# Part of a SwiGLU in-projection computed by seven block products over both token blocks, with weight loads of single pieces

## The chip, the core and the metric

The kernel runs on one core of a Trainium2 chip. The metric is the device time of one execution in microseconds. Time before: median 969.24 us of three runs (968.96 to 971.36).

## What is computed

A trunk of two layers on 256 tokens of width 1024, all in float32. Each layer is an FFN, a token mixer and a second FFN, each between two RMSNorms; layer 0 mixes by stick-breaking attention, layer 1 by latent attention with a rotary part. The FFN is what the change touches:

```python
def rms_norm(x, g):
    y = xf * lax.rsqrt(jnp.mean(xf * xf, axis=-1, keepdims=True) + EPS)
    return y * g

def swiglu(x, w_in, w_out):                       # w_in (1024, 2*2816), w_out (2816, 1024)
    gate, up = jnp.split(x @ w_in, 2, axis=-1)
    return (jax.nn.silu(gate) * up) @ w_out

f = swiglu(rms_norm(x, g[0]), ffn_w_in[i, 0], ffn_w_out[i, 0])
x = x + FFN_RESIDUAL_WEIGHT * rms_norm(f, g[1])   # then the mixer, then the second FFN
```

## The kernel before, in words

The 256 tokens are two blocks of 128. Every weight is streamed once from HBM in pieces of 128 rows by up to 512 columns. Precision is kept by taking each operand apart: ACT copies a piece, rounded, to a high part (L345, `split`), DVE subtracts that from the piece to get the low part (L351), and PE makes three products of a piece, high by high, low weight by high token and high weight by low token (`mm3`, recorded at L474). `use` (L585) is these three matmuls for one block; a piece is used by block 0 and later by block 1, then its two `r` slots come free.

An FFN (`ffn`, L617) goes over 11 tiles of 256 columns of gate beside the same 256 of up. For a tile, `project` (L595) sums eight pieces in a PSUM bank; ACT takes SiLU of the gate half, scaled by the norm's factor `rpre` (L634), DVE multiplies it with the scaled up half (L636), PE transposes the product (L482), ACT and DVE take it apart (L492, L512), and `out_rows` multiplies it with four pieces of the second weight into two banks that stay for the whole FFN. `pre_norm` (L547) transposes x, multiplies by the gain (L559) and takes the result apart; the norm's factor per token, from two squares on ACT (L540), a sum on DVE (L542) and a power on POOL (L544), is worked out beside it, since only L634 and L636 need it. `post_norm` (L569) scales the output and adds it to x (L578, L581).

The order of all instructions comes from a list scheduler (`Plan.run`, L167): every operation is recorded with an engine, a planned duration and what it reads and writes, and the scheduler places them with finite pools of slots: 76 `r` slots for operand parts, 9 `w` slots for intermediate tiles, 4 `raw` buffers of two pieces each for loads, 8 PSUM banks. Small operations (class 0) go ahead of the stream of pieces (class 1). On PE, block 0 may lead block 1 by a number of pieces that `LEADS` gives for each sub-layer; `CAPS` says how many pieces may be held ready. The loads go through SP's queue in the order of the pieces, each when its raw buffer is free.

## Time and profile before

| | |
|---|---|
| three runs | 969.24 us median (968.96 to 971.36) |
| profiled execution | span 968.2 us; the page gives no other time for it |
| PE, DVE, ACT busy | 956.9, 643.3, 562.7 us |
| granted TensorE clock | 1.00 in every slice, 0.999 in the mean |
| HBM read | 168.15 MB, 175 GB/s over the span, 276 to 280 in the first twentieth |

The span is cut off at the first and the last instruction of the core. Busy shares are averages over stages; the chain of waits tells what the end of the run hung on, and the groups by line tell what the pieces of it cost.

### The profile page before, as it was taken

What the parts mean: (1) busy time and instruction counts of PE and PEld (TensorE: products, weight loads), DVE (VectorE), ACT (ScalarE), POOL (GpSimd) and SP (SyncE); (2) the same over time, 40 slices, a digit from 0 to 9 for tenths busy, and PEclk for the clock granted to TensorE, in tenths of its full rate; (3) what the DMA queues carried; (4) which work ended last, traced back from release to release, by engine and by line L of the source; (5) the groups of instructions that cost most, each with busy time, mean ns of one, the idle gap of its engine ahead of it and who ended that gap; (6) DMA issues with size and microseconds to landing.
All of it is one profiled execution on the core that took longest, in us unless ns stands there. A gap on an engine that the chain in (4) does not pass through costs nothing.

```text
span 968.2 us, 13457 instructions
## 1 busy us (share of the span) xinstructions
PE 956.9 (99%) x4575; PEld 797.1 (82%) x4575; DVE 643.3 (66%) x1214; ACT 562.7 (58%) x1202; POOL 26.2 (3%) x75
## 2 busy tenths in 40 slices
PE   8999999999999999999999999999999999999997
PEld 6778888888888888888888888888899988888885
DVE  7884646678777875645477564556899997555533
ACT  7754535568878764545364453545798776444421
POOL 2000000000000000000000000000200000000000
PEclk9999999999999999999999999999999999999999
DMA  8885665634434385656745656575614178666511
GB/s 276 280 249 184 193 199 184 207 131 153 131 109 153 112 276 176 193 180 188 225 131 174 190 184 192 179 232 168 192 41 131 32 236 278 196 194 188 186 62 44
DMA packets 127974, 170.10 MB, mean 176 GB/s; under 512 B 8768, under 2 KB 109472, under 8 KB 127904
## 3 DMA queue, kind: packets, MB, share of 16 engines
q1 hardware_dynamic: 127792, 169.18, 55.2%
q8 instruction: 36, 0.59, 0.3%
q14 instruction: 34, 0.28, 0.1%
q10 hardware_dynamic: 112, 0.05, 0.0%
HBM read 168.15 MB, written 1.05 MB: 175 GB/s over the span
## 4 chain that ended last, share of the span: by engine, by line
PE 92%; DMA 3%; DVE 2%; ACT 1%; issue 1%; POOL 0%; SPq 0%; DVEq 0%; POOLq 0%; ACTq 0%
PE bank L474 88%; PE bank L482 5%; DMA raw<-in_ffn_w_in_dram 3%; DVE r L351 2%; ACT r L345 1%; SPq L334 0%; DVE w L636 0%; DVE w L559 0%; ACT r L492 0%; DVE x L581 0%; DVEq L1133 0%; ACT junk L540 0%; POOLq L1133 0%; POOL cbuild L299 0%; POOL invf L818 0%
## 5 line engine op out<-in xcount | busy, mean ns | idle before, releaser
L474 PE MATMUL bank<-r,r 128*128 128x512 f32 (+3 forms) x4080 | 926.2, 384 | 0.3 <-ACT r L345 0.2
L474 PEld LDWEIGHTS bank<-r,r 128*128 128x128 f32 (+1 forms) x4080 | 736.7, 188 | 139.5 <-ACT r L345 1.2
L351 DVE TENSOR_TENSOR r<-raw,r 128x512 fp32r<-128x512 f32 (+1 forms) x628 | 400.1, 683 | 42.4 <-ACT r L345 33.1
L345 ACT CAST r<-raw 128x512 fp32r<-128x512 f32 (+1 forms) x628 | 353.9, 616 | 56.8 <-DMA raw<-in_ffn_w_in_dram 26.7
L634 ACT ACTIVATE w<-bank,rpre 128x256 f32<-128x256 f32 x88 | 41.7, 474 | 215.5 <-PE bank L474 215.4
L636 DVE SCALAR_TENSOR_TENSOR w<-bank,rpre,w 128x256 f32<-128x256 f32 x88 | 42.5, 483 | 185.9 <-ACT w L634 185.9
L492 ACT CAST r<-bank 128x256 fp32r<-128x256 f32 (+5 forms) x166 | 64.2, 399 | 75.6 <-PE bank L482 65.7
L512 DVE TENSOR_TENSOR r<-bank,r 128x256 fp32r<-128x256 f32 (+5 forms) x166 | 74.3, 454 | 45.8 <-ACT r L492 44.7
L482 PE MATMUL bank<-ident,w 128*128 128x128 f32 (+1 forms) x326 | 55.0, 272 | 2.1 <-DVE w L636 2.0
L482 PEld LDWEIGHTS bank<-ident,w 128*128 128x128 f32 (+1 forms) x326 | 41.3, 137 | 16.6 <-DVE w L636 4.0
L512 DVE TENSOR_TENSOR r<-w,r 128x512 fp32r<-128x512 f32 x48 | 32.5, 687 | 4.9 <-ACT r L507 2.0
L540 ACT ACTIVATE junk<-bank 128x512 bf16<-128x512 f32 x24 | 14.3, 597 | 22.6 <-PE bank L474 22.5
L578 DVE TENSOR_TENSOR w<-bank,w 128x512 f32<-128x512 f32 x24 | 16.4, 684 | 15.9 <-ACT junk L540 15.7
L544 POOL TENSOR_TENSOR rpost<-ms,half_neg 128x1 f32<-128x1 f32 x12 | 6.6, 548 | 700.0 <-DVE ms L542 700.0
L559 DVE TENSOR_TENSOR w<-bank,gT 128x512 f32<-128x512 f32 x24 | 16.3, 686 | 2.2 <-PE bank L482 2.0
L540 ACT ACTIVATE junk<-x 128x512 bf16<-128x512 f32 x24 | 15.1, 631 | 4.3 <-DVE x L581 2.3
L581 DVE SCALAR_TENSOR_TENSOR x<-w,rpost,x 128x512 f32<-128x512 f32 x24 | 17.1, 745 | 0.4
L482 PE MATMUL bank<-ident,x 128*128 128x128 f32 x96 | 15.0, 297 | 0.0
L482 PEld LDWEIGHTS bank<-ident,x 128*128 128x128 f32 x96 | 12.9, 155 | 1.9 <-issue 0.2
L492 ACT CAST r<-w 128x512 fp32r<-128x512 f32 x20 | 12.2, 619 | 3.6 <-DVE w L559 3.5
L1035 ACT ACTIVATE w<-bank,mx 128x128 f32<-128x128 f32 (+1 forms) x32 | 13.1, 425 | 0.4 <-DVE mx L1031 0.3
L736 DVE SCALAR_TENSOR_TENSOR w<-bank,w 128x512 f32<-128x512 f32 x12 | 8.2, 689 | 4.3 <-ACT w L734 4.1
(85 smaller groups left out, 211.5 us busy)
## 6 DMA issues: line engine op xcount, KB each, us to landing
raw<-in_ffn_w_in_dram SPq DMA_DIRECT2D x352, 256.0 KB, 3.9
...
```

The lines of the kernel that those rows point to most:

```text
L345: h = op("act", act_us(n), lambda: nc.scalar.copy(pc.hi[:, :n], raw[:, off:off + n]), r=rr, w=[(pc.hi, 0)], cls=1, after=splits[-1:], piece=i)
L351: nc.vector.tensor_tensor(out=pc.lo[:, :n], in0=raw[:, off:off + n], in1=pc.hi[:, :n].bitcast(F32), op=ALU.subtract)
L474: nc.tensor.matmul(o, a, b, start=start, stop=stop, skip_group_check=True)
L482: nc.tensor.transpose(o, i, ident[:])
L492: nc.scalar.copy(dst(), src())
L512: nc.vector.tensor_tensor(out=dst(), in0=src(), in1=hi().bitcast(F32), op=ALU.subtract)
L540: op("act", act_us(512, 1), lambda src=src, h=h: nc.scalar.activation(junk[:], src(), AF.Square, scale=scale, accum_out=ss[:, h:h + 1]), r ...
L559: op("dve", dve_us(512), lambda h=h, y=y, tr=tr: nc.vector.tensor_tensor(out=y[:].rearrange("p (k t) -> p k t", t=P), in0=tr[:].rearrange( ...
L578: op("dve", dve_us(512), lambda h=h, t=t: nc.vector.tensor_mul(out=t[:], in0=acc[h][:], in1=g[h][:]), r=[(acc[h], 0), (g[h], 0)], w=[(t, 0 ...
L581: op("dve", dve_us(512) + 0.06, lambda h=h, t=t: nc.vector.scalar_tensor_tensor(xt[b][h][:], t[:], k.rpost[:], xt[b][h][:], op0=ALU.mult, ...
L634: op("act", act_us(FT, 1), lambda o=o, hid=hid: nc.scalar.activation(hid[:, 0:FT], o[:, 0:FT], AF.Silu, scale=k.rpre[:]), r=[(o, 0), (k.rp ...
L636: op("dve", dve_us(FT) + 0.06, lambda o=o, hid=hid: nc.vector.scalar_tensor_tensor(hid[:, FT:], o[:, FT:], k.rpre[:], hid[:, 0:FT], op0=AL ...
```

## The change

Two groups of 512 columns of gate and the same 512 of up, 1024 of the 2816, are computed together for both blocks of tokens as a two-by-two block product: tokens by halves of the 1024 inputs, inputs by gate and up. In Strassen's form (the variant with 15 sums) this takes seven block products instead of eight. Each product (`pair_product`) has four pieces, each used once, for both blocks at the same time. For them

- four sums of token operands are made for each FFN (`combos`, DVE), and taken apart by ACT and DVE;
- for each group 16 weight pieces are loaded, DVE makes 16 sums of pieces in place (`total`), and 28 pieces are taken apart instead of 16;
- two PSUM banks gather several products one after another, and ACT copies or DVE sums take the states in between out (`copy_act`, `vec512`).

Since tokens of both blocks are added to each other, the norm's factor must be in them before: `pre_norm` with `scaled=True` works out the factor first, ACT scales x by it (L627 of the changed kernel), and only then come the transposes; SiLU and product lose the factor. The remaining seven tiles, the seven products and the second weight are put in an order by `FFN_ORDER`. Loads take one piece each, into slots of the `w` pool, which grows from 9 to 25 (the four raw buffers go); `r` shrinks from 76 to 68 slots. The stream holds 628 loads where it held 508, of the same bytes. `LEADS`, `CAPS` and other tables have new values, and `AHEAD`, `KEEP` and `RESERVE` limit loads and splits in the scheduler.

```diff
-LEADS = [14, 12, 9, 16, 17, 7]
-CAPS = [28, 29, 23, 22, 32, 23]
-RSLOTS = 76
-WSLOTS = 9
-RAWS = 4
-HOLD = 0.25
-STOCK = 5
+LEADS = [14, 10, 13, 17, 15, 8]
+CAPS = [28, 27, 23, 22, 23, 24]
+RESERVE = [4, 6, 4, 4, 2, 6]
+AHEAD = 9
+KEEP = 12
+RSLOTS = 68
+WSLOTS = 25
+HOLD = 0.26
+STOCK = 7
 X1_AT = 1
 WARM_A = 4
 WARM_B = 4
+PAIR = 512
+FFN_ORDER = ("i0 i1 o0 s0.0 s0.1 s0.2 s0.3 o1 s0.4 s0.5 s0.6 i2 i3 s1.0 t0.0 s1.1 t0.1 s1.2 t0.2 s1.3 t0.3 s1.4 o2 "
+             "s1.5 o3 s1.6 i4 t1.0 t1.1 i5 t1.2 t1.3 i6 o4 o5 o6")
...
+                    if o.first is not None and (
+                            o.first - self.split_pos >= AHEAD or
+                            len(self.free["w"]) < KEEP):
+                        continue
+                    if o.debt > 0 and (self.held >= CAPS[o.phase] or
+                                       len(self.free["r"]) - self.debt < 2 + RESERVE[o.phase]):
                         continue
                     cand.append((max(o.ready, self.slots_ready(o), self.bank_ready(o, e), at[e]), o))
...
-        raw = Buf("raw")
...
+    def load(view, src, size):
+        raw = Buf("w")
+        o = op("dma", size / 360e3, lambda: nc.sync.dma_start(view(raw), src), w=[(raw, 0)], cls=1, after=stream[-1:])
+        o.first, o.phase = len(pieces), phase[0]
+        stream.append(o)
         return raw
...
+    def add_pair(kind, w, q, c0, raws):
+        def fetch(nm):
+            c = c0 + (FF if nm[1] == "2" else 0)
+            raws[nm] = [add_rows(kind, w, (int(nm[0]) - 1) * 512, k, c, PAIR) for k in range(4)]
+        def total(dst, src, neg=False):
+            for d, t in zip(raws[dst], raws[src]):
+                def fn(d=d, t=t):
+                    if neg:
+                        nc.vector.scalar_tensor_tensor(d[:], d[:], -1.0, t[:], op0=ALU.mult, op1=ALU.subtract)
+                    else:
+                        nc.vector.tensor_add(out=d[:], in0=d[:], in1=t[:])
+                op("dve", dve_us(PAIR), fn, r=[(d, 0), (t, 0)], w=[(d, 0)], cls=1)
+        def parts(nm):
+            for k in range(4):
+                split(raws[nm][k], kind + (q, k), PAIR)
+        if q == 0:
+            fetch("11")
+            parts("11")
+        elif q == 1:
+            fetch("12")
+            total("11", "12")
+            parts("11")
+        elif q == 2:
+            fetch("22")
+            total("11", "22")
+            total("12", "22")
+            parts("11")
+        elif q == 3:
+            parts("22")
+        elif q == 4:
+            parts("12")
+        elif q == 5:
+            fetch("21")
+            total("11", "21", True)
+            parts("21")
+        else:
+            parts("11")
...
-        for j in range(NJ + 1):
-            if j < NJ:
-                add_in2(("in", l, f, j), ffn_w_in[l, f], j * FT, FF + j * FT, FT)
-            if j >= 1:
-                add_rows(("out", l, f, j - 1), ffn_w_out[l, f], (j - 1) * FT, (l, f, j) == (1, 1, NJ))
+        w, w2 = ffn_w_in[l, f], ffn_w_out[l, f]
+        raws = {}
+        last = [i for i in FFN_ORDER.split() if i[0] in "ot"][-1]
+        for item in FFN_ORDER.split():
+            kind, n = item[0], item[1:]
+            if kind == "i":
+                add_in2(("in", l, f, int(n)), w, FF, AT[item], FT)
+            elif kind == "o":
+                add_out(("out", l, f, int(n)), w2, AT["i" + n], item == last and (l, f) == (1, 1))
+            elif kind == "s":
+                p, q = n.split(".")
+                add_pair(("pair", l, f, int(p)), w, int(q), AT["s" + p], raws.setdefault(p, {}))
...
+    def pre_norm(b, l, i, scaled=False):
         k = blocks[b]
         gi = (l * 6 + i) * KC
-        k.xh, k.xl = [Buf("r"), Buf("r")], [Buf("r"), Buf("r")]
+        k.xh, k.xl, k.y = [Buf("r"), Buf("r")], [Buf("r"), Buf("r")], [Buf("w"), Buf("w")]
+        if scaled:
+            stats(b, 0)
         for h in range(2):
-            y, tr = Buf("w"), Buf("bank")
-            def turn(h=h, tr=tr):
+            y, tr = k.y[h], Buf("bank")
+            xs = xt[b][h]
+            if scaled:
+                xs = Buf("w")
+                op("act", act_us(512, 1), lambda h=h, xs=xs: nc.scalar.activation(
+                    xs[:], xt[b][h][:], AF.Copy, scale=k.rpre[:]), r=[(xt[b][h], 0), (k.rpre, 0)], w=[(xs, 0)])
+            def turn(xs=xs, tr=tr):
                 for c in range(4):
-                    transpose(tr[:, c * P:(c + 1) * P], xt[b][h][:, c * P:(c + 1) * P])
-            k.turned = op("pe", 4 * pe_us(P), turn, r=[(xt[b][h], 0)], w=[(tr, 0)])
+                    transpose(tr[:, c * P:(c + 1) * P], xs[:, c * P:(c + 1) * P])
+            k.turned = op("pe", 4 * pe_us(P), turn, r=[(xs, 0)], w=[(tr, 0)])
...
     def use(b, key, fn, o, r, n):
-        """The products of one piece of a weight."""
-        k = blocks[b]
+        k = blocks[b or 0]
         i = piece_at[key]
         pc = pieces[i]
         k.last = op("pe", 3 * pe_us(n), lambda: fn(pc.hi[:, :n], pc.lo[:, :n]),
-                    r=r + [(pc.hi, 0), (pc.lo, 0)], w=[(o, 0)], cls=1, after=[k.last] if k.last else [], blk=b, piece=i)
+                    r=r + [(pc.hi, 0), (pc.lo, 0)], w=[(o, 0)], cls=1,
+                    after=[q.last for q in ([k] if b is not None else blocks) if q.last],
+                    blk=(b,) if b is not None else (0, 1), piece=i)
         k.last.phase = phase_of[i]
+        if b is None:
+            blocks[1].last = k.last
...
+    def combos():
+        (a11, a12), (a21, a22) = blocks[0].y, blocks[1].y
+        (h11, h12), (h21, h22) = blocks[0].xh, blocks[1].xh
+        (l11, l12), (l21, l22) = blocks[0].xl, blocks[1].xl
+        a5, a6, a3, a7 = (Buf("w") for _ in range(4))
+        par = {}
+        for nm, d, x, y, o in (("a5", a5, a22, a21, ALU.subtract), ("a7", a7, a11, a21, ALU.add),
+                               ("a6", a6, a5, a11, ALU.subtract), ("a3", a3, a12, a6, ALU.add)):
+            op("dve", dve_us(512), lambda d=d, x=x, y=y, o=o: nc.vector.tensor_tensor(
+                out=d[:], in0=x[:], in1=y[:], op=o), r=[(x, 0), (y, 0)], w=[(d, 0)], cls=0.6)
+            h, lo = Buf("r"), Buf("r")
+            op("act", act_us(512), lambda d=d, h=h: nc.scalar.copy(h[:], d[:]), r=[(d, 0)], w=[(h, 0)], cls=0.6)
+            op("dve", dve_us(512), lambda d=d, h=h, lo=lo: nc.vector.tensor_tensor(
+                out=lo[:], in0=d[:], in1=h[:].bitcast(F32), op=ALU.subtract), r=[(d, 0), (h, 0)], w=[(lo, 0)], cls=0.6)
+            par[nm] = (h, lo)
+        return [(h11, l11), par["a5"], par["a6"], par["a3"], par["a7"], (h12, l12), (h22, l22)]
...
+    def pair_product(l, f, p, q, st):
+        if not st:
+            st.update(Z=Buf("bank"), W=Buf("bank"), Y=Buf("bank"), s1=Buf("w"), s2=Buf("w"), m5=Buf("w"))
+        o = {0: "Z", 1: "W", 2: "Z", 3: "W", 4: "Z", 5: "Y", 6: "Z"}[q]
+        first, last = q in (0, 1, 5), q in (6, 3, 5)
+        xh, xl = par_now[0][q]
+        o = st[o]
+        for kc in range(4):
+            c = slice(kc * P, (kc + 1) * P)
+            use(None, ("pair", l, f, p, q, kc), lambda wh, wl, c=c, kc=kc: mm3(
+                o[:], xh[:, c], xl[:, c], wh, wl, first and kc == 0, last and kc == 3), o, [(xh, 0), (xl, 0)], 512)
+        if q == 0:
+            copy_act(st["s1"], o, [(o, 0)], [(st["s1"], 0)])
+        elif q == 1:
+            copy_act(st["m5"], o, [(o, 0)], [(st["m5"], 0)])
+        elif q == 2:
+            copy_act(st["s2"], o, [(o, 0)], [(st["s2"], 0)])
+        elif q == 3:
+            st["up0"] = Buf("w")
+            vec512(st["up0"], o, st["s2"], ALU.subtract)
+        elif q == 4:
+            st["up1"] = Buf("w")
+            vec512(st["up1"], o, st["m5"], ALU.subtract)
+        elif q == 5:
+            g = Buf("w")
+            vec512(g, o, st["s1"], ALU.add)
+            pair_hidden(0, p, g, 1.0, st["up0"])
+        else:
+            pair_hidden(1, p, o, -1.0, st["up1"])
...
-    for b in range(NB):
-        for l in range(2):
-            ffn(b, l, 0)
+    for l in range(2):
+        ffn(l, 0)
+        for b in range(NB):
             if l == 0:
                 sb_mixer(b)
             else:
                 mla_mixer(b)
-            ffn(b, l, 1)
+        ffn(l, 1)
```

The rows of a listing below stand in the order in which an engine takes its instructions.

On DVE at the start of the program, from the low parts of block 0's tokens to the third low part of a weight (L351 before, L366 in the changed kernel; L559 and L634 are gain multiplications, L512 and L574 low parts of tokens, L738 sums of tokens and L742 their low parts). Before:

```order
L512 TENSOR_TENSOR r_62<-w_139,r_61 128x512
L512 TENSOR_TENSOR r_65<-w_140,r_63 128x512
L351 TENSOR_TENSOR r_67<-raw_146,r_64 128x512
L351 TENSOR_TENSOR r_69<-raw_146,r_66 128x512
L351 TENSOR_TENSOR r_71<-raw_147,r_68 128x512
L351 TENSOR_TENSOR r_72<-raw_147,r_70 128x512
L559 TENSOR_TENSOR w_141<-bank_155,gT 128x512
L542 TENSOR_SCALAR msx_203<-ssx_202 128x1
L559 TENSOR_TENSOR w_142<-bank_156,gT 128x512
L512 TENSOR_TENSOR r_75<-w_141,r_73 128x512
L351 TENSOR_TENSOR r_77<-raw_148,r_74 128x512
```

Now, from the low part of block 1's tokens on:

```order
L574 TENSOR_TENSOR r_77<-w_148,r_74 128x512
L738 TENSOR_TENSOR w_151<-w_138,w_148 128x512
L574 TENSOR_TENSOR r_80<-w_150,r_78 128x512
L738 TENSOR_TENSOR w_152<-w_150,w_148 128x512
L742 TENSOR_TENSOR r_83<-w_151,r_81 128x512
L738 TENSOR_TENSOR w_130<-w_152,w_138 128x512
L738 TENSOR_TENSOR w_131<-w_142,w_130 128x512
L742 TENSOR_TENSOR r_87<-w_152,r_85 128x512
L742 TENSOR_TENSOR r_89<-w_130,r_86 128x512
L366 TENSOR_TENSOR r_92<-w_133,r_66 128x512
L742 TENSOR_TENSOR r_94<-w_131,r_90 128x512
L366 TENSOR_TENSOR r_96<-w_134,r_68 128x512
```

Before, four low parts of weights stood between block 0's tokens and block 1's gain; now the first two stand ahead of all of this, and the third comes behind both blocks' tokens and seven of the eight operations for the sums.

On DVE where block 1 goes from the first mixer into the second FFN (L578 and L653 are the products of the post-norm, L581 and L656 the additions to x, L351 and L366 low parts of weights). Before:

```order
L351 TENSOR_TENSOR r_80<-raw_146,r_117 128x512
L351 TENSOR_TENSOR r_118<-raw_146,r_107 128x512
L351 TENSOR_TENSOR r_97<-raw_147,r_135 128x512
L578 TENSOR_TENSOR w_143<-bank_156,w_140 128x512
L542 TENSOR_SCALAR ms_200<-ss_199 128x1
L578 TENSOR_TENSOR w_139<-bank_157,w_141 128x512
L581 SCALAR_TENSOR_TENSOR x_189<-w_143,rpost_201,x_189 128x512
L581 SCALAR_TENSOR_TENSOR x_189<-w_139,rpost_201,x_189 128x512
L636 SCALAR_TENSOR_TENSOR w_137<-bank_152,rpre_198,w_137 128x256
L559 TENSOR_TENSOR w_144<-bank_151,gT 128x512
L542 TENSOR_SCALAR msx_203<-ssx_202 128x1
```

Now:

```order
L420 TENSOR_TENSOR w_146<-w_146,w_151 128x512
L366 TENSOR_TENSOR r_126<-w_142,r_82 128x512
L420 TENSOR_TENSOR w_151<-w_151,w_138 128x512
L653 TENSOR_TENSOR w_145<-bank_156,w_144 128x512
L604 TENSOR_SCALAR ms_204<-ss_203 128x1
L653 TENSOR_TENSOR w_140<-bank_158,w_148 128x512
L656 SCALAR_TENSOR_TENSOR x_193<-w_145,rpost_205,x_193 128x512
L656 SCALAR_TENSOR_TENSOR x_193<-w_140,rpost_205,x_193 128x512
L420 TENSOR_TENSOR w_142<-w_142,w_131 128x512
L710 TENSOR_TENSOR w_150<-bank_160,w_150 128x256
L366 TENSOR_TENSOR r_108<-w_149,r_89 128x512
L604 TENSOR_SCALAR msx_207<-ssx_206 128x1
```

Here the sums of weight pieces for the first group of products (L420) have come in among block 1's norms; in DVE's order some of them stand behind a row that waits for block 1.

On ACT at the same place (L540 and L602 squares, L345 and L359 high parts of weights, L492 and L554 high parts of others). Before:

```order
L540 ACTIVATE junk,ss_199<-bank_156 128x512
L540 ACTIVATE junk,ss_199<-bank_157 128x512
L634 ACTIVATE w_137<-bank_152,rpre_198 128x256
L540 ACTIVATE junk,ssx_202<-x_189 128x512 x2
L492 CAST r_129<-bank_155 128x256
L492 CAST r_82<-w_144 128x512
L492 CAST r_102<-w_145 128x512
L345 CAST r_123<-raw_147 128x512
L345 CAST r_136<-raw_148 128x512
L345 CAST r_65<-raw_148 128x512
L345 CAST r_78<-raw_149 128x512
```

Now:

```order
L602 ACTIVATE junk,ss_203<-bank_156 128x512
L359 CAST r_89<-w_149 128x512
L602 ACTIVATE junk,ss_203<-bank_158 128x512
L602 ACTIVATE junk,ssx_206<-x_193 128x512
L708 ACTIVATE w_150<-bank_160 128x256
L602 ACTIVATE junk,ssx_206<-x_193 128x512
L554 CAST r_71<-bank_155 128x256
L627 ACTIVATE w_153<-x_193,rpre_208 128x512
L627 ACTIVATE w_152<-x_193,rpre_208 128x512
L554 CAST r_76<-w_139 128x512
L554 CAST r_84<-w_134 128x512
```

Between the squares of x (`ssx`) and the rounding of the normed tokens there are now two scalings (L627) that read the factor.

## Rows read from the trace of the kernel before

**Rows 1.** Part 1 of the page: busy us (share of the span) and instructions of each engine.

```profile
PE 956.9 (99%) x4575; PEld 797.1 (82%) x4575; DVE 643.3 (66%) x1214; ACT 562.7 (58%) x1202; POOL 26.2 (3%) x75
```

**Rows 2.** Chain that ended last, in order of time: start us, us, what.

```profile
81.54 14.99 PE bank L474 x66
98.36 14.99 PE bank L474 x66
```

**Rows 3.** Groups by line, PE: form, count | busy us, mean ns | idle before.

```profile
L474 PE MATMUL bank<-r,r 128*128 128x512 f32 x3672 | 870.8, 393 | 0.3 <-ACT r L345 0.2
```

**Rows 4.** Timeline, DVE, start of the run: start us, us, what.

```profile
15.84 3.09 DVE L351 TENSOR_TENSOR r<-raw,r 128x512 fp32r<-128x512 f32 x5
23.55 3.69 DVE L351 TENSOR_TENSOR r<-raw,r 128x512 fp32r<-128x512 f32 x6
```

**Rows 5.** Groups by line, DVE and ACT, columns as in rows 3.

```profile
L351 DVE TENSOR_TENSOR r<-raw,r 128x512 fp32r<-128x512 f32 x612 | 391.9, 686 | 41.8 <-ACT r L345 32.4 <-ACT w L731 0.6 <-PE bank L474 0.6
L636 DVE SCALAR_TENSOR_TENSOR w<-bank,rpre,w 128x256 f32<-128x256 f32 x88 | 42.5, 483 | 185.9 <-ACT w L634 185.9
L512 DVE TENSOR_TENSOR r<-bank,r 128x256 fp32r<-128x256 f32 x96 | 40.6, 422 | 40.4 <-ACT r L492 39.8
L506 DVE CAST r<-w 128x512 fp32r<-128x512 f32 x10 | 4.2, 425 | 0.7 <-ACT w L749 0.4
L345 ACT CAST r<-raw 128x512 fp32r<-128x512 f32 x612 | 346.5, 619 | 55.8 <-DMA raw<-in_ffn_w_in_dram 26.7 <-DMA raw<-in_ffn_w_out_dram 14.8 <-PE bank L474 8.7
```

**Rows 6.** Windows: us, busy PE, PEld, DVE, ACT, POOL (instructions), clock, DMA share, GB/s.

```profile
290.00:387.00 97.00, 97.00 (x472) 81.27 (x471) 69.86 (x123) 63.68 (x129) 2.19 (x4) 1.00 0.57 178
...
700.00:760.00 60.00, 60.00 (x407) 55.73 (x406) 58.63 (x148) 53.52 (x163) 4.03 (x9) 1.00 0.26 77
```

**Rows 7.** Timeline, first 20 us, DVE and ACT.

```profile
4.11 0.63 ACT L540 ACTIVATE junk<-x 128x512 bf16<-128x512 f32 x1 [1.57 <-DMA x<-in_x_dram]
5.41 0.19 ACT L540 ACTIVATION_READ_ACCUMULATOR junk<-x 128x1 f32 x1
5.68 0.69 DVE L559 TENSOR_TENSOR w<-bank,gT 128x512 f32<-128x512 f32 x1 [0.59 <-PE bank L482]
14.63 2.49 DVE L351 TENSOR_TENSOR r<-raw,r 128x512 fp32r<-128x512 f32 x4
18.91 0.47 ACT L634 ACTIVATE w<-bank,rpre 128x256 f32<-128x256 f32 x1 [0.20 <-PE bank L474]
```

**Rows 8.** Timeline, PE, the three waits of the ramp.

```profile
35.33 0.44 PE L482 MATMUL bank<-ident,w 128*128 128x128 f32 x2 [0.34 <-DVE w L636]
45.11 0.44 PE L482 MATMUL bank<-ident,w 128*128 128x128 f32 x2 [1.16 <-DVE w L636]
62.66 0.44 PE L482 MATMUL bank<-ident,w 128*128 128x128 f32 x2 [0.48 <-DVE w L636]
```

**Rows 9.** Waits of SP's queue: who waited for whom, us, times, longest.

```profile
SPq L334 <- DVE r L351: 629.8, 283, 23.7
```

**Rows 10.** End of the run: chain, then windows as in rows 6.

```profile
957.03 4.80 PE bank L474 x21
...
964.00:965.00 1.00, 0.00 (x0) 0.00 (x0) 1.00 (x2) 0.00 (x0) 0.00 (x0) 1.00 0.00 0
965.00:966.00 1.00, 0.00 (x0) 0.00 (x0) 0.00 (x0) 0.00 (x0) 0.00 (x0) 0.68 0.82 303
966.00:967.00 1.00, 0.00 (x0) 0.00 (x0) 0.00 (x0) 0.00 (x0) 0.00 (x0) 0.50 0.59 221
```

**Rows 11.** Timeline around 333 us, ACT, POOL and DVE: block 1's norms.

```profile
330.10 0.60 ACT L540 ACTIVATE junk<-bank 128x512 bf16<-128x512 f32 x1
334.84 0.55 POOL L544 TENSOR_TENSOR rpre<-msx,half_neg 128x1 f32<-128x1 f32 x1 [3.11 <-DVE msx L542]
333.88 0.69 DVE L559 TENSOR_TENSOR w<-bank,gT 128x512 f32<-128x512 f32 x1 [0.31 <-PE bank L482]
334.81 1.14 ACT L492 CAST r<-w 128x512 fp32r<-128x512 f32 x2
```

More of the change, by code (lines that the diff above doesn't have):

```diff
@@ L96 @@
 class Op:
[L97 removed]
+    __slots__ = ("eng", "us", "fn", "cls", "deps", "users", "wait", "bufs", "ready", "end", "table", "blk", "piece", "alt", "phase", "debt", "first")
 class Plan:
     def __init__(self, pools, set_table):
[L104 removed]
+        self.free = {tag: [(0.0, i) for i in range(len(pools[tag]))] for tag in pools}
         self.tiles = pools
@@ L133, in op @@
         o.ready, o.end = 0.0, None
+        o.debt = 0
+        o.first = None
         for b in o.bufs:
```

240 lines of the change are left out of this document (145 added, 95 removed).

## Prediction

> **What bounds the kernel now.** The page's first part comes first: PE is busy 956.9 of 968.2 us, DVE 643.3, ACT 562.7 [rows 1]. A busy PE need not be a PE at its pace, so the chain of waits in order of time is read next: it runs through 66 matmuls of 512 columns in 14.99 us, and the same again 16.82 us later, again and again [rows 2]. That is 0.2271 us for one, and it is the price of every matmul below. The groups by line give their number: 3672 of this shape, 834 of the 968 us, with 0.3 us of idle time ahead of them [rows 3]. The rest of the chain is transposes, smaller products and the two ends. So the kernel is as long as PE's list of matmuls; DVE and ACT only have to stay ahead of it. How fast they can be is read from stretches in which they run without a gap: five DVE subtractions of 512 columns take 3.09 us and six 3.69, so one follows the other after 0.60 us though each is shown with 0.69 [rows 4].
>
> **PE's list.** The listing of the changed program has 3576 matmuls of that shape, 96 fewer: 12 for each of two groups of columns in four FFNs (84 instead of 96 for 512 columns of gate and of up on both blocks). 96 x 0.2271 = 21.8 us less. The stationary and moving shapes are the same and so is the number of transposes (422), so the pace should be too. The Trainium skill, page "TensorE: Matmul & The Clock Gate", section "Back-to-back issue gap", gives about 131 ns as the sustained spacing of 512-column matmuls in a real kernel; by that the saving would be 12.6 us, an estimate from that page. The chain here shows 227 ns and decides [rows 2].
>
> **DVE and ACT.** Added on DVE, by the listing: 96 low parts of weights, 128 sums of weight pieces, 16 sums of token operands and their 16 low parts, 40 sums and products of 512 columns behind the seven products, 16 wider low parts; gone are 32 products and 32 low parts of 256 columns. No row shows a sum of two weight pieces; the nearest is the subtraction of the same shape, 0.686 us each, and the shortest that a row of 512 columns has is the cast's 0.425 [rows 5]. Of 0.43 to 0.69 I take 0.69, since a sum reads two operands as the subtraction does. 312 x 0.69 - 32 x 0.48 - 32 x 0.42 = +186 us: DVE goes from 643 to about 829 us, 87% of a 952 us span, ACT by the same count (184 of 512 columns at 0.62 more, 64 narrower ones at about 0.42 less) from 563 to 650. On average both stay below PE. Evidence that such a share can be carried: from 700 to 760 DVE is busy 58.6 of 60 us and PE 60.0 [rows 6].
>
> The average hides one place. In the second FFN, between the last low part of o0 and that of product s0.6, DVE has 65 instructions of 512 columns and 7 of 256 (32 low parts, 16 sums of weights, block 1's norms, the eight operations for the sums of tokens): 65 x 0.60 + 7 x 0.34 = 41.4 us. PE has 108 matmuls between the same points, 24.5 us. The deficit of 17 us has to come out of pieces prepared earlier; in the other three FFNs it is 7, 15 and 15. In the second group of products the two lists are level (39 against 42). Before the first group PE spends 27 us on i0, i1 and o0 with each piece used by both blocks, in which DVE needs 12 us for their low parts, and some twenty pieces can lie ready. So I take the deficit as covered, at 0, and keep its 53 us in all as the upper bound of a rival.
>
> **The start.** The factor of the norm now multiplies the tokens ahead of the transposes. Ahead of the eighth low part of a weight DVE now has eight more operations (four sums of tokens, four low parts of them) and three casts of 0.42, which is 8 x 0.60 + 3 x 0.34 = 5.8 us. That eighth part ended at 16.5 (third of the four from 14.63) [rows 7]; the first gain multiplication moves from 5.68 to about 7.9 (squares done at 5.60 [rows 7], sum and power 0.8, scaling 0.62, four transposes and the handovers 0.9), of which two low parts that now come first take up 1.2. So 16.5 + 5.8 + 1.0 = 23.3, and block 0's first tile is done by 23.5 instead of 18.7, when ACT's first SiLU started after 0.20 us of idle time [rows 7]. PE does 0.7 us more for block 1 meanwhile: 4.1 us lost. Against that stand three waits of PE later in the ramp, 0.34, 1.16 and 0.48 us [rows 8], while ACT waited 26.7 us for loads [rows 5] and each load for a free buffer [rows 9]. Single pieces in 25 shared slots are issued at least 10 us of DVE work ahead of their use once the start is over; I credit the 2.0 us. Net +2.1. The 120 more transfers cost SP about 0.4 us each, on a queue that waits 630 us for DVE [rows 9]: nothing.
>
> ACT's list ahead of block 1's last scaling holds four squares with read-out (0.75), four copies (0.52, the 0.62 of [rows 5] less the overlap) and three more scalings: 4.11, the first square's start, plus 4 x 0.75 + 4 x 0.52 + 4 x 0.62 is 11.7. With the transposes PE's first product starts at about 12.3, and its 12 matmuls with the first two pieces end at 15.0. The third piece's low part, six operations ahead of the eighth, comes at 19.7: a gap of 4.7 us. At the end of the run, behind the last matmul at 961.83, the granted clock was still 1.00 from 964 to 965, 0.68 in the next microsecond and 0.50 after it [rows 10], the lower of the two levels, 1.2 GHz. A gap of 4.7 us may thus bring the lower level. It costs nothing if the clock holds; if the nine matmuls of three pieces run at 512 columns / 1.2 GHz = 0.43 us, it costs 9 x 0.2 = 1.8. I take 1.0. The same page of the Trainium skill, section "What's actually happening", says that the gate is throttled by default and opens with recent activity; by that the full 1.8 would be paid and the sum be 0.8 us higher, an estimate.
>
> **Between stages.** Block 0's and block 1's norms ahead of an FFN get longer: power, scaling and transposes in a row, where the factor was needed only behind the first tile. At the end of the mixer of layer 0, block 1's last product is done at 330.10, its factor at 335.39, and the first rounded operand at 335.4, from a gain multiplication at 333.88 that did not wait for the factor [rows 11]. Now: 335.39 + scaling 0.62 + four transposes 0.5 + from the multiplication's start to the cast's end 1.55 = 338.1, that is 8.0 us after the last product. PE's list holds 24 matmuls and 10 transposes of 0.12 ((16.82 - 72 x 0.2271) / 4 [rows 2]) between those two points, 6.7 us: 1.3 us uncovered. Block 0's chain is of the same make, and the list has 8.1 us for it. At the other two joints that lead into an FFN the list holds 10.1 to 13.3 us, which covers it. I take +2.0 for both, bounds 0 (nothing queued) and 4 (each chain a further 1 us in DVE's and ACT's queues).
>
> **Sum.** -21.8 + 2.1 + 1.0 + 2.0 = -16.7 us. The profiled span is 968.2; the three runs have the median 969.24, 1.04 above it for what lies around the span, which the change leaves alone. 969.24 - 16.7 = **952.5 us**.
>
> **Rivals.** *Nothing lost*: the start hides behind the loads, the joints hold. For it, PE ran without a gap through the stretch of this joint before [rows 6]. 969.24 - 21.8 - 2.0 = 945.4. *DVE lets through a little*: in three FFNs some 3 us of the deficit reach PE, with norm chains waiting in DVE's order: 952.5 + 9 = 961.5. For it speaks the 17 us, against it rows 6. *DVE becomes the bound* (the other side): in the first group of products the prepared pieces run out, since token operands and their sums hold 16 of 68 operand slots and joint products pull both blocks to the same place. If half of the 53 us stays uncovered, 952.5 + 27 = 979. It decides the sign when more than 17 us is uncovered, under 9 us of lead in each FFN. Against it: DVE full for 60 us without a gap on PE [rows 6]. *The matmuls taken out are worth less than the mean spacing*, down to the mean weight load, 797.1 / 4575 = 0.174 us [rows 1]: 969.24 - 16.7 + 5.1 = 957.6; no stretch of the chain shows it. The Trainium skill's 131 ns (same page and section as above) would make that 961.7, an estimate. That fewer matmuls are not issued is excluded by the listing.
>
> **Chances.** Forecast (949 to 956) 0.50, nothing lost 0.15, a little let through 0.19, matmuls worth less 0.02, DVE as bound 0.14, of which 0.05 ends within 0.3% and 0.09 slower. 0.3% (2.9 us) is about what a measurement of this kernel can tell from no change. Faster 0.86, same 0.05, slower 0.09. The range reaches from the case without loss to the little let through with both upper bounds of the start and the joints: 946 to 966, 0.86 of the cases.
>
> **What would show it.** PE: 3576 matmuls of 512 columns at 227 ns in the chain. Start: a PE gap near 15 to 20 us, the first SiLU near 23.5, a clock under 1.00 just behind it. Second FFN: PE waits of a few us near its start, none in the later ones. DVE near 830 us busy. The forecast is wrong if PE shows repeated waits for DVE's low parts or sums in the first group of products, or if matmuls take another pace.

## The result, and the profile after

| | us, median (range) | ratio to before (95%) |
|---|---|---|
| before | 969.41 (968.96 to 971.36) | |
| changed | 963.78 (962.35 to 964.47) | 0.9928 (0.9908 to 0.9947) |

The change makes the kernel 5.6 us faster. 16.7 were forecast; the time lies between 946 and 966, but outside the forecast's 949 to 956, and the size is a third. The profiled execution took 962.35 us with a span of 960.6, 7.5 less than the 968.2 before. Device time is 1.7 us above the span in all runs that give both, not 1.04 as the prediction had it. So the profiled execution of the kernel before was about 0.5 us above its median and that of the changed kernel 1.4 below: the traces show 1.9 us more of a gain than the medians do, and that much of the 11.1 us by which the forecast missed lies outside what they can explain. Two of the four runs of the changed kernel were 1.3 to 2.1 us longer than the other two, at a mean clock of 0.995 instead of 0.998, and neither of them was traced.

Part 1 of the page of the changed kernel [rows 1], two rows of its chain of waits (start us, us, what) [rows 2], and four groups by line (form, count | busy us, mean ns | idle before) [rows 3, 5]:

```profile
PE 938.0 (98%) x4479; PEld 778.9 (81%) x4479; DVE 789.9 (82%) x1464; ACT 633.5 (66%) x1322; POOL 29.2 (3%) x75
```

```profile
46.97 26.55 PE bank L536 x117
...
97.87 34.70 PE bank L536 x153
```

```profile
L536 PE MATMUL bank<-r,r 128*128 128x512 f32 x3576 | 845.9, 393 | 6.0 <-DVE r L366 3.9 <-DVE r L574 1.1 <-ACT r L554 0.8
L544 PE MATMUL bank<-ident,w 128*128 128x128 f32 x326 | 55.1, 281 | 7.5 <-ACT w L627 7.2 <-DVE w L710 0.2
...
L420 DVE TENSOR_TENSOR w<-w,w 128x512 f32<-128x512 f32 x96 | 62.0, 682 | 0.0
...
L418 DVE SCALAR_TENSOR_TENSOR w<-w,w 128x512 f32<-128x512 f32 x32 | 21.7, 681 | 0.0
```

96 matmuls are gone, and the pace is 26.55 / 117 = 0.227 us as before. The idle time ahead of them grew from 0.3 to 6.0 us, and ahead of transposes (L544) PE waits 7.2 us for the scaled tokens (L627), which the kernel before did not have. L420 and L418 are the 128 sums of weight pieces.

To see where time went I went through PE's matmuls of each trace (one execution of each kernel) in order of time, priced each by its columns (0.2271 us for 512, 0.119 for 256, 0.12 for 128) and took the sum from the time at which the last of them ended. What is left is time in which PE did not work at its pace, whether the profile shows it as idle or as slow matmuls. By stretch, in us ("FFN2" is the second of the four FFNs, "FFN3" the third; a "joint" is the place where one stage ends and the next begins on PE; the kernels from e1 to e14 come in the experiments):

```
kernel               list    start   first mixer   FFN2 to FFN3   the rest   last matmul
                          0 to 120   to FFN2 joint        joint               ends
before              951.7     10.9        -0.1           -0.1       -0.6        961.82
changed             929.9     16.2         5.7            1.4        1.1        954.29
e5_sep_loads        951.7      8.3         0.0            1.5        0.9        962.34
e4_sep_scaled       951.7     13.0         3.2            5.3        1.3        974.43
e3_unscaled         929.9     15.0         0.2            1.9        0.9        947.94
e8_unscaled_late    929.9      8.3         0.0            1.8        0.7        940.84
e1_sums_late        929.9     11.7         5.8            1.4        1.0        949.76
e2_warm_gap         933.8     12.3         5.7            0.1        1.2        953.05
e7_no_wsums         929.9     18.7         4.7            1.4        0.7        955.34
e9_more_ahead       929.9     12.1         2.6            0.5        0.8        945.90
e11_lead            929.9     10.8         0.6            1.7        0.9        943.94
e12_one_group       940.8     11.2         2.6            5.8        1.2        961.53
e14_after_pow       929.9     17.9         8.0            0.8        2.3        958.85
e13_pow_alone       929.9     11.2         0.4            1.1        2.2        944.79
```

The list fell by 21.8 us (96 matmuls at the forecast's price, which the chain confirms), and 14.3 came back where 5.1 were expected: 5.3 at the start, 5.8 at the joint of the first mixer and FFN2, 1.5 at the next joint, 1.7 elsewhere. Inside the FFNs, product groups included, PE loses nothing.

**The start.** PE's timeline (start us, us, what, [idle time before <- who ended it]), then ACT's first scaling (L627) with what stands ahead of it, then DVE's rows ahead of the third low part (at 20.68), then windows (us, busy PE, PEld, DVE, ACT, POOL (instructions), granted clock, DMA share, GB/s):

```profile
10.18 1.11 PE L544 MATMUL bank<-ident,w 128*128 128x128 f32 x4 [0.89 <-ACT w L627]
11.09 1.48 PE L536 MATMUL bank<-w 128*128 128x512 bf16 x3
12.37 1.06 PE L544 MATMUL bank<-ident,w 128*128 128x128 f32 x4
...
14.25 3.22 PE L536 MATMUL bank<-r,r 128*128 128x512 f32 x13
21.42 9.61 PE L536 MATMUL bank<-r,r 128*128 128x512 f32 x35 [3.94 <-DVE r L366]
```

```profile
6.14 1.35 ACT L359 CAST r<-w 128x512 fp32r<-128x512 f32 x2 [0.74 <-DMA w<-in_ffn_w_in_dram]
7.40 0.72 ACT L627 ACTIVATE w<-x,rpre 128x512 f32<-128x512 f32 x1
```

```profile
17.55 0.68 DVE L742 TENSOR_TENSOR r<-w,r 128x512 fp32r<-128x512 f32 x1
18.15 1.41 DVE L738 TENSOR_TENSOR w<-w,w 128x512 f32<-128x512 f32 x2
19.48 1.28 DVE L742 TENSOR_TENSOR r<-w,r 128x512 fp32r<-128x512 f32 x2
20.68 0.68 DVE L366 TENSOR_TENSOR r<-w,r 128x512 fp32r<-128x512 f32 x1
```

```profile
18.00:20.00 2.00, 0.00 (x0) 0.00 (x0) 1.97 (x4) 1.77 (x5) 0.00 (x0) 1.00 1.03 344
20.00:22.00 2.00, 0.58 (x1) 0.50 (x2) 2.00 (x5) 2.00 (x6) 0.00 (x0) 0.74 1.01 366
22.00:24.00 2.00, 2.00 (x6) 1.60 (x5) 2.00 (x4) 2.00 (x5) 0.00 (x0) 0.50 1.05 396
24.00:26.00 2.00, 2.00 (x9) 1.61 (x9) 2.00 (x4) 1.98 (x4) 0.00 (x0) 0.90 1.05 391
```

The first scaling stands behind two weight pieces that ACT rounds first (L359). The first product starts at 14.25, not 12.3: four transposes take 1.1 us here, not 0.5, and matmuls on zeros, which the kernel before has too, stand between them on PE. PE then waits 3.94 us for a low part behind sums of tokens (L738) and their low parts (L742). Behind that wait the clock is at its lower level, 1.2 GHz (0.50 from 22 to 24), and 35 matmuls take 9.61 us, 0.275 each.

**The joint of the first mixer and FFN2.** PE's waits; some of block 0's chain on ACT and DVE (L602 is a square of x, L604 the sum, L627 the scaling; L927 and L929 belong to block 1's attention, L359 rounds weights); and block 1's chain on ACT, DVE and POOL (its last product ended at 331.7) [rows 11]:

```profile
315.46 0.66 PE L544 MATMUL bank<-ident,w 128*128 128x128 f32 x4 [0.64 <-ACT w L627]
...
319.19 9.46 PE L536 MATMUL bank<-r,r 128*128 128x512 f32 x46 [1.06 <-DVE r L574]
...
338.28 1.27 PE L544 MATMUL bank<-ident,w 128*128 128x128 f32 x8 [0.97 <-ACT w L627]
340.37 8.02 PE L536 MATMUL bank<-r,r 128*128 128x512 f32 x33 [0.82 <-ACT r L554]
```

```profile
312.53 0.62 ACT L602 ACTIVATE junk<-x 128x512 bf16<-128x512 f32 x1
313.32 0.21 DVE L604 TENSOR_SCALAR msx<-ssx 128x1 f32<-128x1 f32 x1
313.14 0.62 ACT L927 ACTIVATE w<-w 128x512 f32<-128x512 f32 x1
313.66 1.13 ACT L359 CAST r<-w 128x512 fp32r<-128x512 f32 x2
314.69 1.34 ACT L627 ACTIVATE w<-x,rpre 128x512 f32<-128x512 f32 x2
313.79 0.69 DVE L929 SCALAR_TENSOR_TENSOR w<-bank,w 128x512 f32<-128x512 f32 x1 [0.26 <-ACT w L927]
```

```profile
331.73 0.60 ACT L602 ACTIVATE junk<-bank 128x512 bf16<-128x512 f32 x1 [0.24 <-PE bank L536]
336.26 0.21 DVE L604 TENSOR_SCALAR msx<-ssx 128x1 f32<-128x1 f32 x1
336.61 0.86 POOL L606 TENSOR_TENSOR rpre<-msx,half_neg 128x1 f32<-128x1 f32 x1 [3.25 <-DVE msx L604]
337.50 1.33 ACT L627 ACTIVATE w<-x,rpre 128x512 f32<-128x512 f32 x2 [0.48 <-POOL rpre L606]
339.70 1.24 ACT L554 CAST r<-w 128x512 fp32r<-128x512 f32 x2 [0.86 <-DVE w L634]
```

From 331.7 to 340.37 are 8.7 us, against 8.0 forecast. Block 0 has i0, i1 and o0 (two separate tiles, and the second weight of the first) to do meanwhile and no more: the next item, a product, needs both blocks. Of the 5.7 us that the table has here, 2.5 are lost by 320, in the waits for block 0's tokens, 2.6 between 330 and 345, in those for block 1's, and some 0.5 just behind.

### The profile page after: what moved, and what is told of

It reads as the page before. It is cut to its first block, busy times and chain, and to the rows that moved or that the text cites. A ratio compares the mean times of both kernels' runs of the same rounds, so it can differ in the third digit from the quotient of the medians.

```text
span 960.6 us, 14255 instructions
## 1 busy us (share of the span) xinstructions
PE 938.0 (98%) x4479; PEld 778.9 (81%) x4479; DVE 789.9 (82%) x1464; ACT 633.5 (66%) x1322; POOL 29.2 (3%) x75
## 4 chain that ended last, share of the span: by engine, by line
PE 89%; DVE 6%; ACT 3%; issue 1%; POOL 1%; DMA 0%; SPq 0%; POOLq 0%; DVEq 0%; ACTq 0%
PE bank L536 84%; PE bank L544 4%; DVE r L366 1%; DVE r L574 1%; DVE x L656 1%; ACT junk L602 1%; ACT w L627 1%; ACT r L359 0%; POOL rpre L606 0%; DVE w L738 0%; DMA w<-in_ffn_w_in_dram 0%; DVE r L742 0%; ACT r L554 0%; DVE w L634 0%; ACT w L1228 0%
## 5 line engine op out<-in xcount | busy, mean ns | idle before, releaser
L536 PE MATMUL bank<-r,r 128*128 128x512 f32 (+2 forms) x3984 | 900.0, 383 | 6.0 <-DVE r L366 3.9
L536 PEld LDWEIGHTS bank<-r,r 128*128 128x128 f32 (+1 forms) x3984 | 719.3, 188 | 143.0 <-DVE r L366 4.4
L366 DVE TENSOR_TENSOR r<-w,r 128x512 fp32r<-128x512 f32 (+1 forms) x724 | 456.1, 681 | 22.4 <-PE bank L536 10.1
L359 ACT CAST r<-w 128x512 fp32r<-128x512 f32 (+1 forms) x724 | 401.4, 618 | 61.8 <-DVE w L420 30.9
L554 ACT CAST r<-bank 128x256 fp32r<-128x256 f32 (+5 forms) x150 | 61.7, 425 | 58.7 <-PE bank L544 52.6
L708 ACT ACTIVATE w<-bank 128x256 f32<-128x256 f32 x56 | 21.5, 383 | 108.4 <-PE bank L536 105.1
L574 DVE TENSOR_TENSOR r<-bank,r 128x256 fp32r<-128x256 f32 (+5 forms) x150 | 71.4, 484 | 21.5 <-ACT r L554 20.6
L710 DVE TENSOR_TENSOR w<-bank,w 128x256 f32<-128x256 f32 x56 | 23.6, 422 | 63.8 <-ACT w L708 62.8
L544 PE MATMUL bank<-ident,w 128*128 128x128 f32 (+1 forms) x390 | 63.3, 280 | 7.9 <-ACT w L627 7.2
L544 PEld LDWEIGHTS bank<-ident,w 128*128 128x128 f32 (+1 forms) x390 | 48.5, 141 | 24.9 <-ACT w L627 10.7
L420 DVE TENSOR_TENSOR w<-w,w 128x512 f32<-128x512 f32 x96 | 62.0, 682 | 0.0
L574 DVE TENSOR_TENSOR r<-w,r 128x512 fp32r<-128x512 f32 x48 | 32.2, 686 | 4.4 <-ACT r L569 3.3
L653 DVE TENSOR_TENSOR w<-bank,w 128x512 f32<-128x512 f32 x24 | 16.4, 683 | 19.5 <-ACT junk L602 19.5
L602 ACT ACTIVATE junk<-bank 128x512 bf16<-128x512 f32 x24 | 14.4, 600 | 26.8 <-PE bank L536 26.8
L418 DVE SCALAR_TENSOR_TENSOR w<-w,w 128x512 f32<-128x512 f32 x32 | 21.7, 681 | 0.0
L634 DVE TENSOR_TENSOR w<-bank,gT 128x512 f32<-128x512 f32 x24 | 16.0, 684 | 2.4 <-PE bank L544 2.2
L751 DVE TENSOR_TENSOR w<-bank,w 128x512 f32<-128x512 f32 x24 | 16.5, 686 | 1.8 <-PE bank L536 1.6
L656 DVE SCALAR_TENSOR_TENSOR x<-w,rpost,x 128x512 f32<-128x512 f32 x24 | 16.9, 746 | 1.1
L602 ACT ACTIVATE junk<-x 128x512 bf16<-128x512 f32 x24 | 15.1, 630 | 3.9 <-DVE x L656 2.2
L748 ACT COPY w<-bank 128x512 f32<-128x512 f32 x24 | 14.1, 587 | 2.2 <-PE bank L536 1.7
```

The costliest lines, as they stand in the source:

```text
L359: h = op("act", act_us(n), lambda: nc.scalar.copy(pc.hi[:, :n], raw[:, :n]), r=[(raw, 0)], w=[(pc.hi, 0)], cls=1, after=splits[-1:], piece=i)
L366: nc.vector.tensor_tensor(out=pc.lo[:, :n], in0=raw[:, :n], in1=pc.hi[:, :n].bitcast(F32), op=ALU.subtract)
L418: nc.vector.scalar_tensor_tensor(d[:], d[:], -1.0, t[:], op0=ALU.mult, op1=ALU.subtract)
L420: nc.vector.tensor_add(out=d[:], in0=d[:], in1=t[:])
L536: nc.tensor.matmul(o, a, b, start=start, stop=stop, skip_group_check=True)
L544: nc.tensor.transpose(o, i, ident[:])
```

## The experiments

The kernel before was run again beside each set of experiments, and its median lay between 969.1 and 970.2 us. A difference between two experiments of different sets is therefore good to about 1 us; the ratios are each taken to the kernel before of the same set.

**One part alone: loads, factor, products.** Four kernels make a square: eleven separate tiles or products, without or with the factor ahead of the transposes, all with the new loads, pools and tables. The three edits:

```diff
-FFN_ORDER = ("i0 i1 o0 s0.0 s0.1 s0.2 s0.3 o1 s0.4 s0.5 s0.6 i2 i3 s1.0 t0.0 s1.1 t0.1 s1.2 t0.2 s1.3 t0.3 s1.4 o2 "
-             "s1.5 o3 s1.6 i4 t1.0 t1.1 i5 t1.2 t1.3 i6 o4 o5 o6")
+FFN_ORDER = "i0 i1 o0 i2 o1 i3 o2 i4 o3 i5 o4 i6 o5 i7 o6 i8 o7 i9 o8 i10 o9 o10"
...
-        pre_norm(b, l, 4 * f, True)
+        pre_norm(b, l, 4 * f)
...
-                out=d[:], in0=x[:], in1=y[:], op=o), r=[(x, 0), (y, 0)], w=[(d, 0)], cls=0.6)
+                out=d[:], in0=x[:], in1=y[:], op=o), r=[(x, 0), (y, 0)], w=[(d, 0)], cls=1)
```

The first makes all tiles separate (e4 and e5, where `combos` goes too), the second takes the factor out of the tokens (e3, e5, e8; in e5 SiLU and its product take it as in the kernel before, e3 and e8 leave it out altogether), the third, with the same in the two operations behind it, puts the token sums behind the weights' parts (e8, and e1 below).

> The kernel before with the new loads and pools alone: all eleven tiles separately, the factor applied behind them as before, single pieces through 25 shared buffers. Theory (the new loads take away the ramp's waits and cost nothing): 967.0 to 967.8 us, waits for w from DVE between 35 and 46 us gone. Rival (single loads cost, and hide part of the saving in the changed kernel): 969.4 us or more.

970.52 us, ratio 1.0003 (0.9992 to 1.0014): the rival's time. The waits of the ramp [rows 8] are gone, 2.6 us at the start, but 1.6 come back at the joint of FFN2 and FFN3 and 1.5 elsewhere. The new loads bring nothing in the end; the 2.0 us credited to them were real in their place and not kept.

> The norm's factor is left out of the tokens in the four FFNs (squares, sum and power stay, as in the kernel before): transposes no longer wait for it. Products and sums stay. Theory (about 5 us of the 8.5 lost at the three joints and 1.5 to 2 at the start come from the longer chain of power and scaling): 956 to 958 us, PE waits at 315 and 338 us gone or under 0.5 us. Rival (the joints lose because products on both blocks need both blocks' sums, whatever the factor): 961.5 to 963 us with the waits still there.

956.28 us, 0.9855 (0.9833 to 0.9877). The waits at 315 and 338 are gone, the joint loses 0.2 instead of 5.7. At the start little changes, since the token sums still stand ahead of the third low part and the lower clock now lasts longer (0.50 from 18 to 22).

> All eleven tiles separately as in the run with the new loads alone (970.5 us), but with the norm's factor applied to the tokens ahead of the transposes, as the products need it. Theory (the longer chain is paid at the joints only where the products bar block 0 from going on; without them it costs the start some 2 us and the joint of the first mixer to the second FFN at most 2): 972.5 to 974.5 us. Rival (the chain costs its 5 to 6 us at that joint whatever stands behind it): 977 us or more, with PE waits of the same size near it.

981.58 us, 1.0122 (1.0104 to 1.0139): the rival's time. The factor alone, without a product, costs 981.58 - 970.52 = 11.1 us (in the traces 4.7 at the start, 3.2 and 3.8 at the two joints), so the theory's small price is refuted. Where it is paid fits neither. At the first mixer's joint PE has the same waits for block 0's tokens as in the changed kernel (0.65 and 1.07 us, at 317.55 and 321.28), but almost none for block 1's (0.22 at 343.01): there the separate tiles do cover block 1's chain, and 3.2 is less than the rival's 5 to 6. At the next joint PE waits 1.63 and 0.82 us, and the clock is at 0.50 from 534 to 536.

> Token sums behind the weights' parts, and the factor left out of the tokens: both suspected costs away, the products and sums all there. Theory (the start then costs about what it does with the new loads alone, and the first mixer's joint nothing): granted clock 1.00 from 16 us, 949.5 to 951.5 us. Rival (the two costs overlap, so that together they bring less than 5.9 and 7.5): 953 us or more.

949.46 us, 0.9792 (0.9775 to 0.9809), as the theory had it. The start loses 8.3 us, exactly what e5 loses. Against e5, which has tiles in place of the products and the factor behind them, 970.52 - 949.46 = 21.1 us (20.5 by the two ratios): nearly the whole price of 96 matmuls, with all sums of weights and tokens paid for.

**The start.** e1 makes the token sums wait behind the weights' parts. e2 leaves them and puts matmuls on zeros into PE's gap:

```diff
+        if b == 1 and key == ("in", 0, 0, 0, 1):
+            warm(18, [k.last], 0.0)
```

> The 16 token operands of the seven products (sums, casts, low parts) come behind the weights' parts on ACT and DVE, in all four FFNs. Theory (of the 5.4 us lost at the start, the wait of 3.94 us for the third low part and the fall of the clock behind it are the token sums' doing): third low part done near 16.5 instead of 21.4, no PE wait over 1 us there, granted clock 1.00 from 16 to 40, 958 to 959 us. Rival (DVE is full from 16 to 97 us, so the wait only moves to the second product, which needs those sums): a PE wait of 3 to 4 us before the second product and 962 to 964 us.

957.90 us, 0.9872 (0.9846 to 0.9897). PE's timeline and a window of e1, columns as above:

```profile
14.80 10.93 PE L536 MATMUL bank<-r,r 128*128 128x512 f32 x45
```

```profile
20.00:24.00 4.00, 4.00 (x20) 3.30 (x19) 4.00 (x8) 3.98 (x7) 0.00 (x0) 1.00 1.00 351
```

45 matmuls in one go, no wait, the clock at 1.00: 5.9 us (5.4 by the ratios) for a number that sets an order. The wait did not move to the second product.

> 18 matmuls on zeros behind the first twelve real ones of the start, so that PE is busy through its wait; all else in the same order. Theory (the wait itself stays, the clock's lower level behind it is a cost of its own): third low part as before near 21.4, granted clock 1.00 from 16 to 40, 961.4 to 962 us, with runs closer together than 962.3 to 964.5. Rival (DVE sets the pace up to 97 us, the slower matmuls cost nothing): 963.8 us.

961.52 us (961.11 to 963.48), 0.9912 (0.9889 to 0.9935): a time of the theory, but the runs lie no closer together, and they overlap with those of the changed kernel. The clock stays at 1.00, and the 35 matmuls behind the gap take 8.23 us instead of 9.61:

```profile
21.86 8.23 PE L536 MATMUL bank<-r,r 128*128 128x512 f32 x35 [0.20 <-DVE r L366]
```

Yet the profiled execution gains nothing at the start: 12.3 plus 3.9 of added matmuls (933.8 - 929.9) is 16.2 again. Its third low part came 0.44 us later, PE waited for hidden tiles instead, and near 46.5 us both kernels are at the same transposes (46.51 and 46.59). So the 1.4 us that the lower clock took here came to nothing in the end; how much of the 2.3 us between the medians is its doing stays open. A longer stretch has a price: in e7's trace (below) the clock is back at 1.00 from 28 instead of 26, and the start loses 18.7 us instead of 16.2, though its third low part is also 0.5 us later.

**Sums of weights.** e7 drops the DVE operation in `total`.

> The 128 sums of weight pieces are left out (the products take the single pieces), all else as in the changed kernel: DVE does some 77 us less. Theory (these sums lie beside PE's work; they only stand in DVE's queue ahead of a norm's small steps): DVE busy near 715, 962.5 to 963.8 us, the waits at the start and at the joint of 315 to 354 us stay. Rival (DVE's load as such holds the kernel): 958 us or less.

962.91 us (961.27 to 963.40), 0.9928 (0.9913 to 0.9943). DVE is busy 722 us instead of 790 and the time hardly moves, as the theory had it. DVE's load as such does not hold this kernel.

**The joint.** e9 is e1 with more separate work ahead of the products; e11 adds a larger lead in the first mixer; e12 is e9 with one group of products (s and t in an order are a group's seven products and its second weight):

```diff
-FFN_ORDER = ("i0 i1 o0 s0.0 s0.1 s0.2 s0.3 o1 s0.4 s0.5 s0.6 i2 i3 s1.0 t0.0 s1.1 t0.1 s1.2 t0.2 s1.3 t0.3 s1.4 o2 "
+FFN_ORDER = ("i0 i1 o0 i2 o1 s0.0 s0.1 s0.2 s0.3 s0.4 s0.5 s0.6 i3 s1.0 t0.0 s1.1 t0.1 s1.2 t0.2 s1.3 t0.3 s1.4 o2 "
...
-CAPS = [28, 27, 23, 22, 23, 24]
+CAPS = [28, 27, 25, 25, 23, 24]
...
-LEADS = [14, 10, 13, 17, 15, 8]
+LEADS = [14, 16, 13, 17, 15, 8]
```

`CAPS` goes with e9, e11 and e12, `LEADS` with e11 alone. The order of e12:

```diff
+FFN_ORDER = ("i0 i1 o0 i2 o1 s0.0 s0.1 s0.2 s0.3 s0.4 s0.5 s0.6 i3 t0.0 t0.1 i4 t0.2 t0.3 i5 o2 i6 o3 i7 o4 "
+             "i8 o5 o6 o7 o8")
```

> The whole computation, token sums behind the weights' parts (957.9 us), and in each FFN a third separate tile and its second weight ahead of the first product: 36 more matmuls a block, 8 us, that block 0 can do while block 1's factor is worked out; two more pieces may be held. Theory (the products are a bar for block 0, the joint loses what the separate work ahead of it doesn't cover): PE waits from 310 to 350 us under 2 us in all instead of 5.8, 953 to 955 us. Rival (the chain is waited for at its first consumer anyway, or the third tile's pieces aren't prepared in time): 957 us or more.

953.24 us, 0.9831 (0.9816 to 0.9847). Block 1's chain is covered; block 0's remains, at 314.79:

```profile
314.79 9.45 PE L536 MATMUL bank<-r,r 128*128 128x512 f32 x46 [1.07 <-DVE r L574]
```

> The kernel with more separate work ahead of the products (953.2 us), and in the first mixer block 0 may lead block 1 by 16 pieces instead of 10. What is left at its joint is 2.7 us, lost while block 0's own norm is worked out and block 1 has too little of the mixer left. Theory: 6 more pieces of block 1, 18 matmuls or 4.1 us, then lie beside that norm: 950.5 to 951.5 us, no PE wait over 0.4 us from 305 to 320. Rival (what may be held sets the lead, or block 1's last attention steps, not pieces, are what PE waits for): 952.8 us or more.

951.68 us (950.83 to 953.11), 0.9809 (0.9787 to 0.9831), 0.2 above the theory's range: the fastest that does the whole work. The joint loses 0.6 us; the longest PE wait there is 0.23.

> The same kernel (953.2 us, lead 10) with one group of products per FFN instead of two; the other 512 columns as two separate tiles. 48 matmuls more. Theory (a group of products brings the spacing of the matmuls that it leaves out, 12 per FFN at 0.2271 us, and its sums cost PE nothing): 953.2 + 10.9 = 964.1, 963.4 to 964.8 us, DVE busy about 90 us less. Rival (DVE's work for the second group costs PE time somewhere): below 962 us.

968.99 us, 0.9991 (0.9979 to 1.0003), 4.9 us more than the theory, and further from the rival. The list is 10.9 longer, as priced. In the traces, 5.3 more are lost at the joint of FFN2 and FFN3, 5.8 instead of 0.5. Its rows there, PE, POOL and DVE:

```profile
504.15 1.52 PE L544 MATMUL bank<-ident,w 128*128 128x128 f32 x8 [2.28 <-ACT w L627]
```

```profile
500.07 3.27 POOL L606 TENSOR_TENSOR rpre<-msx,half_neg 128x1 f32<-128x1 f32 x1 [2.92 <-DVE msx L604]
```

```profile
499.85 3.09 DVE L366 TENSOR_TENSOR r<-w,r 128x512 fp32r<-128x512 f32 x5
```

A power that took 0.55 us in the kernel before [rows 11] takes 3.27: it begins inside a row of five subtractions of DVE and ends 0.4 us behind the last. PE waits, and the clock is at 0.50 from 506 to 508. So this run does not test what a group of products brings by itself.

**The power on POOL.** In the changed kernel the same happens at 512.7, and in e2, whose DVE and ACT do the same in the same order, it does not:

```profile
512.71 2.07 POOL L606 TENSOR_TENSOR rpre<-msx,half_neg 128x1 f32<-128x1 f32 x1 [2.92 <-DVE msx L604]
```

```profile
512.57 0.86 POOL L606 TENSOR_TENSOR rpre<-msx,half_neg 128x1 f32<-128x1 f32 x1 [2.92 <-DVE msx L604]
```

The first loses 1.4 us at this joint, the second 0.1. The other traces with the scaled factor and two groups agree: where this power takes 2.06 or 2.07 us (e1, e7, e11) the joint loses 1.4 to 1.7, where it takes 0.86 (e9) 0.5. Without the factor in the tokens (e3, e5, e8) the power stands ahead of no transpose, and the joint loses 1.5 to 1.9 by waits for rounded tokens, the cause of which stays open. e14 (the changed kernel) and e13 (e11) let DVE stand still until the power is done:

```diff
+        def both():
+            sums()
+            power()
+            nc.vector.tensor_copy(seen[:], r[:])
```

> The changed kernel with one small DVE copy behind each of the eight sums from which the factors ahead of an FFN come, which reads the factor: DVE stands still until POOL's power is done; all orders else the same. In the runs so far a power took 0.55 us beside a DVE operation with an operand in PSUM, and 0.86 to 3.27 when it began inside one with two operands in SBUF. Theory (DVE's subtractions and sums of SBUF operands hold POOL up, and the 2.07 us of the power near 512.7 are most of the 1.4 us lost at the joint of the second to the third FFN): each of the eight powers 0.55 to 0.6, loss at that joint under 0.4, 962.0 to 963.0 us. Rival (the power's length has another cause, or the stop of DVE costs as much): 963.8 us or more, some powers still 0.86 or longer.

965.91 us, 0.9961 (0.9947 to 0.9975): the rival's time, with no power of 0.86 ahead of an FFN.

> The same copy in the fastest kernel so far (951.7 us), where the power at 501.9 took 2.06 us and the one at 303.6 took 1.46. Theory: loss at the joint of the second to the third FFN under 0.3 instead of 1.4, 950.0 to 951.0 us. Rival: 951.7 us or more.

953.19 us, 0.9830 (0.9815 to 0.9844): the rival's time again. What lengthens the power is shown, the remedy is not one. In both kernels all eight powers ahead of an FFN take 0.55 or 0.56 us, and the waits for the scaled tokens are gone from the joint of FFN2 and FFN3. But that joint still loses 0.8 (e14) and 1.1 (e13) instead of 1.4 and 1.7, not under 0.4 and 0.3; PE now waits 0.26 and 0.28 us for DVE's hidden tiles a little later, and the rest has no cause shown. And both kernels are slower, by 2.1 and 1.5 us. Part of that is DVE's stop: behind a power it stands still for some 0.7 us, and near the last FFN PE waits twice for hidden tiles, 0.55 and 0.45 us in e13, where e11 has no wait. At the first mixer's joint e14 loses 8.0 for 5.7: PE waits 1.69 us for rounded tokens instead of 0.82, and the clock is then at 0.60 and 0.55 from 344 to 348, where the changed kernel has 1.00. Of the 17.9 for 16.2 at e14's start most is not the stop's doing in the trace: the first gain multiplication comes 1.16 us later, since the first scaling stands behind a weight piece that came late (ACT waits 1.32 us for its load).

## Why the prediction was right and wrong

- **PE's list, -21.8: right.** 96 matmuls went at a pace of 0.227 us, and by the step from e5 to e8 the products bring 21.1 with everything they add. 512-column matmuls follow each other at 0.227 us; the 131 ns of the Trainium skill ("TensorE: Matmul & The Clock Gate", "Back-to-back issue gap") would give 12.6 and do not hold for this stream.
- **DVE's deficit in the product groups, 0: right.** No stretch inside an FFN loses time, and 68 us less on DVE (e7) is worth 0.9, no more than two sets of runs differ by. DVE is busy 790 us, not 829: operations in a row take 0.60 us each, and the count took 0.69. Both DVE rivals fall; that the time came near the 961.5 of one of them is chance.
- **The start, +2.1 and +1.0: too low, 5.3.** The loads' credit was 2.6 there, not 2.0, but e5 gives it back later. The factor costs 3.4 (e8 to e1) and the token sums' place in DVE's order 4.5 (e1 to changed); taken the other way round, by e3, the sums cost 6.7 and the factor 1.2. The step that failed placed the third low part at 19.7 and the eighth at 23.3: they came at 21.4 and 25.0, and the first SiLU at 27.7 instead of 23.5. The first gain multiplication was held near 7.9 and came at 9.32, since two weight pieces went ahead of the first scaling on ACT and four transposes took 1.1 us. The gap itself (3.94 for 4.7) and the fall of the clock were as said; the 1.0 for the clock is near the 1.4 of e2's 35 matmuls.
- **Between stages, +2.0: the step that failed most.** 5.8 at one joint, 1.5 at a joint held to be covered, and 1.7 elsewhere, 9.0 in all; the 1.7 are spread over the run, and their cause stays open. Three things were missed. Block 0's chain is not "of the same make": with block 1's attention between its steps on ACT and DVE, it takes from 308.2 to 319.19, 11.0 us, where the prediction saw a list of 8.1 and nothing uncovered; 2.5 us are lost, and a larger lead brings most of them back (e11). Block 1's list was counted right, 24 matmuls and 10 transposes, but its chain takes 8.7 us instead of 8.0, and 2.6 are lost for 1.3; more separate work ahead of the products brings them back (e9). And a power on POOL can take 2 us, which by e2 is most of the 1.5 at the next joint.
- **The mechanism by medians:** products -21.1 (970.5 to 949.5), factor ahead of the transposes +8.4 (to 957.9), token sums ahead of the weights' parts +5.9 (to 963.8), loads +0.3, each good to about 1 us. By e3 instead of e1 the factor is +7.5 and the sums are +6.8. The forecast had -21.8, some +7 for the second and third together, and -2.0.
